# Split-operand gate and numerator products, a DRAM hop for the last gate chunk, and another order of the first weights in a two-layer hybrid trunk

## The chip, the core and the metric

The kernel runs on one core of a Trainium2 chip. The metric is the device time of one execution in microseconds (us), taken as the median of several runs. TensorE (PE) does the matrix products, VectorE (DVE) and ScalarE (ACT) the elementwise work, GpSimd (POOL) some elementwise work and the issue of some transfers, SyncE (SP) issues most transfers. All arrays are float32 in DRAM.

## What is computed

The reference is a trunk of two layers over 256 tokens of width 2048. Cut to what matters here:

```python
for i in range(2):
    hn = rmsnorm(h, norm[i])
    if i == 0:                                   # even layer
        qa, fa, ia, za, xb, zb = split(hn @ e_w_in)
        ya = head_rmsnorm(hgrn2(qa, fa, ia, lb), a_norm) * silu(za)
        xc = causal_conv(xb, b_conv_w, b_conv_b)
        r  = sigmoid(blockwise(xc, w_r) + b_r)   # 8 blocks of 128x128
        ig = sigmoid(blockwise(xc, w_i) + b_i)
        a  = exp(-8 * r * softplus(-lam))
        yb = scan(a, sqrt(1 - a * a) * (ig * xc)) * silu(zb)
        mix = concat(ya, yb) @ e_w_out
    else:                                        # odd layer, mLSTM with 8 heads
        qk, v, og, z, ig, fg = split(hn @ o_w_in)
        q, k = silu(causal_conv(qk))
        num = (q k^T * weights) @ v ; den = row sums of (q k^T * weights)
        yc = head_rmsnorm(num / den, c_norm) * sigmoid(og) * silu(z)
        mix = yc @ o_w_out
    h = h + mix
    h = h + sigmoid(h @ ple_gate_w[i]) * rmsnorm(p[i] @ ple_w[i], ple_norm[i])
out = rmsnorm(h, final_norm)
```

The "gates" of the change are the products of xc with w_r and w_i. The "numerators" are num, with den as one column more.

## The kernel before

**The large products.** TensorE takes float32 operands in two ways here. Plain float32 tiles are multiplied as they are. The large projections instead split each operand into a rounded part `hi` and the rest `lo`, both of type fp32r, and add three products, hi hi + hi lo + lo hi. `load_weights` (L119) fetches a half megabyte (128x1024) at a time into `raw` (5 buffers), casts it on ACT into `whi` (L131) and subtracts on VectorE into `wlo` (L132); whi and wlo have 4 buffers each, and a quarter of a chunk of weights is two such halves. Activations are split in the same way into tiles tagged `ahl` (12 buffers).

`block` (L154) makes one 128-feature block of an even-layer projection, features on partitions: 16 matmuls of 512 columns (L161) and 16 of 256 columns (L167). `quarter_tok` (L214) makes a quarter of a 512-column chunk, tokens on partitions: for each of two token halves 12 matmuls of 512 columns (L225 to L227). `project_tok` runs the four quarters of a chunk; `chunks` and `project_two` (L199, L209) run the first two chunks of a projection in the order (0,0) (0,1) (0,2) (1,0) (1,1) (1,2) (0,3) (1,3), chunk first, quarter second, and call `before(kq)` ahead of each; `ready` (L406) then steps the generator that makes activations 2kq and 2kq+1 until they exist.

**The order of the side work.** All else is written as Python generators in named lanes. `start` puts one into a lane, `step` runs it to its next `yield`, `drain` to its end. `pump` (L74) steps every lane once; it is called in the middle of each `block` and each quarter, so a yield is worth one block or quarter (about 5.5 us). What a pump issues is queued behind the latest matmul, cast and subtraction on their engines. A framework orders the instructions of each engine by priority and sets the semaphores; the casts and subtractions of weights have a raised priority.

**The parts that are touched.**

- Start: `embed` (L317) multiplies p by the first embedding weights. Its first half megabyte comes in four pieces, its second in two, alternating between the queues of ACT and SP; the third and fourth come whole on SP's queue. Then follow the parameters, and x in four chunks of half a megabyte (`load_x`, L479), each scaled and split by ACT (L286) and VectorE (L287), and the weights of the first projection (`in_ei`). The embedding's results are copied out of PSUM into `pl` (L347, L349).
- Gates: `rg_lru` (L809) runs twice (r = 0, 1), in a lane of its own. It loads 128x1024 gate weights `bw`, yields, and then issues 8 plain float32 matmuls a half (L823), four to a yield, each read by a sigmoid.
- Mixer gate of the even layer: `feature_major` (L515) takes a gated chunk from tokens to features: two VectorE transposes of 32x32 blocks (L520), a write to DRAM and four reads back on POOL's queue (`across`, L504, with `lag` yields), and copies on ACT and splits. The odd layer uses it for the first three of four chunks; the last goes through `feature_major_pe` (L531) with 8 TensorE transposes (L542), and all four are drained before the output projection `out_proj` (L413) begins.
- Numerators: `mix(j)` (L1038) runs for four pairs of heads. It makes the weights `wt` (from a pool of 4 tiles of 128x1024, `room`), the scores (L1058, L1059) times these weights in a second tile `scw`, and then the plain float32 products with v (L1070, L1072), with a column of ones as the 257th for den.

Of the kernel before, what the change touches and what calls it, by code (L numbers as in the profile page):

```python
# [11 lines left out]
F32 = mybir.dt.float32  # L12
# [31 lines left out]
def trunk(ctx: ExitStack, tc: tile.TileContext, a, out):  # L44
# [73 lines left out]

    def load_weights(src, pieces=(1, 1), queues=(sy,)):  # L119
        parts = []  # L120
        for hf in range(2):
            raw = wp.tile([P, 1024], F32, name="raw", tag="raw", bufs=5)
            hi = wp.tile([P, 1024], F32R, name="whi", tag="whi")
            lo = wp.tile([P, 1024], F32R, name="wlo", tag="wlo")
            n = 1024 // pieces[hf]
            for c in range(0, 1024, n):
                r, h, l = (x[:, c:c + n] for x in (raw, hi, lo))
                queues[c // n % len(queues)].dma_start(out=r, in_=src[:, hf * 1024 + c:hf * 1024 + c + n])
                with ExitStack() as order:
                    order.enter_context(tc.high_priority(offset=400))  # L130
                    last["act"] = s.copy(h, r).ins  # L131
                    last["dve"] = v.tensor_tensor(out=l, in0=r, in1=h.bitcast(F32), op=ALU.subtract).ins  # L132
            parts.append((hi, lo))
        return parts
# [379 lines left out]

    def feature_major(u, gain, first, y, room):  # L515

        w = room("w")
        w5 = w.rearrange("p (j c h t) -> p h c j t", j=4, c=4, h=2)
        for hf in range(2):
            v.transpose(w5[:, hf], u[:, hf].rearrange("p (c j q) -> p c j q", c=4, j=4))  # L520
        r = room("r")
        yield from across(w, r, f"du{gain}{first}", 5)
        r5 = r.rearrange("p (i c h t) -> p c h i t", i=4, c=4, h=2)
        for b in range(2):
            x = tp.tile([P, 512], F32, name="xr", tag="hn", bufs=3)
            for k in range(2):
                s.activation(x[:, k * T:(k + 1) * T].rearrange("p (h i t) -> p h i t", h=2, i=4), r5[:, 2 * b + k],
                             AF.Copy, scale=pc(gain, first + 2 * b + k))
            y[first // 2 + b] = split_act(x, "y")

    def feature_major_pe(u, gain, first, y):  # L531

        yield
        yield
        banks = []
        for b in range(2):
            ps = px.tile([P, 512], F32, name="mx", tag="mx")
            for k in range(2):
                c = (2 * b + k) * P
                for hf in range(2):  # L540
                    o = k * T + hf * P
                    te.transpose(ps[:, o:o + P], u[:, hf, c:c + P], ident)  # L542
            banks.append(ps)
        yield
        for b, ps in enumerate(banks):
            hi, lo, both = act_pair()
            for k in range(2):
                scaled_split(ps[:, k * T:(k + 1) * T], gain, first + 2 * b + k, hi[:, k], lo[:, k])
            y[first // 2 + b] = (hi, lo, both)

# [54 lines left out]
    with m0_scope:  # L605
# [203 lines left out]
        def rg_lru(r, xc):  # L809
# [6 lines left out]
            if r:  # L816
                yield
            for j in range(2):
                for w, (dst, bias) in enumerate(((av, "bbr"), (it, "bbi"))):
                    ps = px.tile([P, 512], F32, name="mx", tag="mx")  # L820
                    for i in range(2):
                        c = 2 * j + i
                        te.matmul(ps[:, i * T:(i + 1) * T], bw[:, w, c * P:(c + 1) * P], xc[:, c * T:(c + 1) * T],  # L823
                                  start=True, stop=True)
                    for i in range(2):
# [90 lines left out]
    drain("pl")  # L916
    act = out_proj(hq, a["eo"], y, "fe")
    drain("pg")
# [29 lines left out]
    with tc.tile_pool(name="m1", bufs=2) as m1:  # L948
# [38 lines left out]

        VW = 257
        vts = []
# [48 lines left out]
        def mix(j):  # L1038
# [24 lines left out]
            vt = vts[j]  # L1063
            nm = m1.tile([P, 2, 512], F32, name="num", tag="vt", bufs=6)
            for i in range(2):
                pool, tag = ((px, "mx"), (pst, "st"))[i]
                for hf in range(2):
                    c = hf * 8 + 2 * j + i
                    ps = pool.tile([P, 512], F32, name="nu", tag=tag)[:, 0:VW]
                    te.matmul(ps, scw[:, i, hf * P:(hf + 1) * P], vt[:, 0, i], start=True, stop=(hf == 0))  # L1070
                    if hf:
                        te.matmul(ps, scw[:, i, T:384], vt[:, 1, i], start=False, stop=True)  # L1072
                    o = nm[:, hf, i * 256:(i + 1) * 256]
                    s.copy(o, ps[:, 0:256])
                    v.tensor_copy(den[:, c:c + 1], ps[:, 256:VW])
                    sq = tp.tile([P, 512], F32, name="sq", tag="sq")[:, 0:256]
# [19 lines left out]
        for j in range(4):  # L1096
            psv = project_tok(a["ov"], j, acth)
            vt = m1.tile([P, 2, 2, VW], F32, name="vt", tag="vt", bufs=6)
            gp.memset(vt[:, :, :, 256:VW], 1.0)
            for hf in range(2):  # L1100
                s.activation(vt[:, hf, :, 0:256], psv[hf].rearrange("p (i e) -> p i e", i=2), AF.Copy,
                             scale=norm["rt"][:, hf:hf + 1])
            vts.append(vt)
            for c in (j // 2, 2 + j // 2):
                drain(f"qk{c}")
            start("mix", mix(j))
# [15 lines left out]
        for j in range(4):  # L1122
            u = m1.tile([P, 2, 512], F32, name="u", tag="vt", bufs=6)
            gate_tok(a["oz"], j, acth, u)
            for hf in range(2):
                for i in range(2):
# [234 lines left out]
```

## Time and profile before

| | |
|---|---|
| Median of 3 runs | 1051.79 us (1050.85 to 1053.89) |
| The profiled execution's own time | 1051.14 us |
| Its span, first to last instruction | 1049.4 us |
| Granted TensorE clock | 0.998 |
| Moved by DMA | 225.40 MB, mean 215 GB/s |

The profile comes from one execution. Its views: the busy time of each engine; the chain of work that ended last, followed back from the last instruction; groups of instructions by line, operation and tile, with busy time and mean duration; the waits; a timeline; the busy time of each engine in given stretches. Times are us from the first instruction. PE and PEld are TensorE's matmuls and its weight loads, a trailing q an engine's sequencer. Matmuls overlap, so the durations of single matmuls add up to more than the time they take.

### The profile page before, as it was taken

How to read it: one execution, taken by the hardware profiler on the slowest of the kernel's cores; microseconds unless marked ns; L12 is line 12 of the kernel's file. 1: busy time of each engine (PE TensorE's matmuls, PEld its weight loads, DVE VectorE, ACT ScalarE, POOL GpSimd, SP SyncE). 2: the span in 40 equal slices, each digit the busy share in tenths (PEclk: the TensorE clock that was granted, in tenths of full speed). 3: DMA queues.
4: the chain of work that ended last, by engine and by line, in shares of the span. 5: the costliest groups of instructions: out<-in, count | busy, mean ns of one | idle time of the engine just before them, and what ended most of it. 6: DMA issues, size and time to landing. Idle time of an engine off the chain costs nothing.

```text
span 1049.4 us, 14961 instructions
## 1 busy us (share of the span) xinstructions
PE 1038.6 (99%) x5504; PEld 869.1 (83%) x5504; DVE 724.3 (69%) x1085; ACT 594.3 (57%) x893; POOL 114.4 (11%) x162
## 2 busy tenths in 40 slices
PE   9999999999999999999999999999999999999996
PEld 7888888888888888887888788888888888888886
DVE  6857897997877666766569864454457767666675
ACT  7775545869654444565557765544445565444553
POOL 0001232522201111111021000000001110111000
PEclk9999999999999999999999999999999999999999
DMA  9865544545867877687597644446557775977652
GB/s 350 311 205 192 172 164 157 182 150 192 275 234 258 249 247 230 212 277 235 177 271 248 203 169 160 161 161 201 199 188 225 250 262 187 294 239 242 201 181 81
DMA packets 64587, 225.40 MB, mean 215 GB/s; under 512 B 8065, under 2 KB 9345, under 8 KB 64513
## 3 DMA queue, kind: packets, MB, share of 16 engines
q1 hardware_dynamic: 55440, 196.38, 56.5%
q0 software_dynamic: 8496, 27.27, 8.6%
q8 instruction: 43, 0.70, 0.3%
q10 hardware_dynamic: 576, 0.79, 0.2%
q14 instruction: 32, 0.25, 0.1%
HBM read 211.30 MB, written 13.11 MB: 214 GB/s over the span
## 4 chain that ended last, share of the span: by engine, by line
PE 97%; DMA 1%; ACT 1%; DVE 0%; issue 0%; SPq 0%; ACTq 0%
PE mm L225 22%; PE mm L226 22%; PE mm L227 22%; PE mm L161 11%; PE mm L167 6%; PE mx L225 2%; PE mx L227 2%; PE mx L226 2%; PE mm L338 1%; DMA xq<-in_xT_dram 1%; PE mm L1196 1%; PE mm L1195 1%; PE mm L1194 1%; PE mx L823 1%; PE nu L1070 1%; PE mx L661 0%
## 5 line engine op out<-in xcount | busy, mean ns | idle before, releaser
L132 DVE TENSOR_TENSOR wlo<-raw,whi 128x1024 fp32r<-128x1024 f32 (+1 forms) x364 | 439.9, 1220 | 246.4 <-ACT whi L131 211.3
L131 ACT CAST whi<-raw 128x1024 fp32r<-128x1024 f32 (+1 forms) x364 | 378.3, 1043 | 356.4 <-PE mm L227 254.8
L225 PE MATMUL mm<-whi,ahl 128*128 128x512 f32 x1024 | 401.5, 392 | 0.0
L227 PE MATMUL mm<-whi,ahl 128*128 128x512 f32 x1024 | 398.5, 389 | 0.0
L226 PE MATMUL mm<-wlo,ahl 128*128 128x512 f32 x1024 | 398.4, 389 | 0.0
L225 PEld LDWEIGHTS mm<-whi,ahl 128*128 128x128 f32 x1024 | 192.2, 188 | 42.0 <-issue 2.1
L227 PEld LDWEIGHTS mm<-whi,ahl 128*128 128x128 f32 x1024 | 192.2, 188 | 40.5
L226 PEld LDWEIGHTS mm<-wlo,ahl 128*128 128x128 f32 x1024 | 192.3, 188 | 39.8 <-DVE wlo L132 0.5
L161 PE MATMUL mm<-ahl,whi 128*128 128x512 f32 x512 | 122.1, 390 | 0.0
L161 PEld LDWEIGHTS mm<-ahl,whi 128*128 128x128 f32 x512 | 94.2, 188 | 18.3
L167 PE MATMUL mm<-ahl,wlo 128*128 128x256 f32 x512 | 67.7, 285 | 0.0
L167 PEld LDWEIGHTS mm<-ahl,wlo 128*128 128x128 f32 x512 | 64.9, 191 | 2.2
L225 PE MATMUL mx<-whi,ahl 128*128 128x512 f32 x96 | 37.5, 391 | 0.0
L227 PE MATMUL mx<-whi,ahl 128*128 128x512 f32 x96 | 37.4, 389 | 0.0
L226 PE MATMUL mx<-wlo,ahl 128*128 128x512 f32 x96 | 37.3, 389 | 0.0
L507 POOL DMA_DIRECT2D ducn<-w x3 | 1.7, 561 | 206.2 <-DVE w L520 206.2
L173 ACT COPY sm<-mm 128x256 f32<-128x256 f32 x32 | 11.7, 366 | 19.1 <-PE mm L167 19.0
L225 PEld LDWEIGHTS mx<-whi,ahl 128*128 128x128 f32 x96 | 18.0, 188 | 3.7
L227 PEld LDWEIGHTS mx<-whi,ahl 128*128 128x128 f32 x96 | 18.0, 188 | 3.8
L226 PEld LDWEIGHTS mx<-wlo,ahl 128*128 128x128 f32 x96 | 18.0, 188 | 3.7
L971 DVE SCALAR_TENSOR_TENSOR qk<-xr,prm,qk 128x255 f32<-128x255 f32 (+2 forms) x48 | 20.4, 475 | 0.6 <-ACT qk L968 0.5
L1195 PE MATMUL mm<-wlo,ahl 128*128 128x256 f32 x64 | 18.1, 283 | 0.0
(304 smaller groups left out, 877.3 us busy)
## 6 DMA issues: line engine op xcount, KB each, us to landing
raw<-in_ew_dram SPq DMA_DIRECT2D x64, 512.0 KB, 4.4
raw<-in_g_dram SPq DMA_DIRECT2D x56, 512.0 KB, 4.7
raw<-in_eo_dram SPq DMA_DIRECT2D x32, 512.0 KB, 4.8
raw<-in_oqk_dram SPq DMA_DIRECT2D x32, 512.0 KB, 4.6
raw<-in_ov_dram SPq DMA_DIRECT2D x32, 512.0 KB, 3.8
raw<-in_oog_dram SPq DMA_DIRECT2D x32, 512.0 KB, 3.7
raw<-in_oz_dram SPq DMA_DIRECT2D x32, 512.0 KB, 4.2
raw<-in_oo_dram SPq DMA_DIRECT2D x32, 512.0 KB, 4.5
```

The costliest lines, as they stand in the source:

```text
L131: last["act"] = s.copy(h, r).ins
L132: last["dve"] = v.tensor_tensor(out=l, in0=r, in1=h.bitcast(F32), op=ALU.subtract).ins
L161: last["pe"] = te.matmul(ps, parts[k // 8][0][:, c:c + P], act[k // 2][2][:, (k % 2) * 512:(k % 2 + 1) * 512], start=(k == 0), stop=False).ins
L167: last["pe"] = te.matmul(ps[:, T:2 * T], parts[k // 8][1][:, c:c + P], act[k // 2][0][:, k % 2], start=False, stop=(k == KT - 1)).ins
L173: s.copy(small, ps[:, T:2 * T])
L225: te.matmul(ps[hf], xh, wh, start=(k == 0), stop=False)
L226: te.matmul(ps[hf], xh, wl, start=False, stop=False)
L227: last["pe"] = te.matmul(ps[hf], xl, wh, start=False, stop=(k == KT - 1)).ins
L338: last["pe"] = te.matmul(ps[hf], tokens(pact[x], k, hf), (hi, lo)[y][:, k * 512:(k + 1) * 512], start=(n == mine[0]), stop=(n == mine[-1]) ...
L823: te.matmul(ps[:, i * T:(i + 1) * T], bw[:, w, c * P:(c + 1) * P], xc[:, c * T:(c + 1) * T], start=True, stop=True)
L971: v.scalar_tensor_tensor(dst[:, sh:T], pi[:, 0:T - sh], pc("ccw", k * 16 + n), dst[:, sh:T], op0=ALU.mult, op1=ALU.add)
L1195: te.matmul(ps[hf], xh, wl, start=False, stop=False)
```

## The change

- Gates: the gate weights are split into a whi and a wlo tile and xc into two ahl tiles, with one yield more, and each product becomes three (`mm3`, L149).
- Numerators: scores are written over `wt`; their split goes into two tiles of the same pool; v is split as it leaves PSUM (`vl` in an ahl tile), and the width becomes 258; each product becomes three, the third with 256 columns.
- The last gate chunk of the odd layer goes through `feature_major`, like the others; `feature_major_pe` goes. The output projection of the odd layer runs through `chunks` and `ready`, in place of a drain of all four.
- `feature_major` gets a `lag`. The even layer uses 4, with a yield ahead of its transposes; the odd layer keeps 5.
- First weights: pieces 0 and 1 on ACT's queue, pieces 2 and 3 and the second half megabyte on SP's, and the third half megabyte in two pieces.

```diff
-    def load_weights(src, pieces=(1, 1), queues=(sy,)):
+    def load_weights(src, pieces=(1, 1), queues=8 * (sy,)):
...
-                queues[c // n % len(queues)].dma_start(out=r, in_=src[:, hf * 1024 + c:hf * 1024 + c + n])
+                queues[hf * 4 + c // n].dma_start(out=r, in_=src[:, hf * 1024 + c:hf * 1024 + c + n])
...
-            parts = load_weights(w[b], *(((4, 2), (s, sy)) if head else ()))
+            parts = load_weights(w[b], *((((4, 2), (s, s) + 6 * (sy,)) if head else ((2, 1),)) if first else ()))
...
-    def out_proj(hq, w, y, lane):
+    def out_proj(hq, parts, lane):
...
-        for c in range(4):
-            ps = project_tok(w, c, y)
+        for c, ps in enumerate(parts):
...
-    def feature_major(u, gain, first, y, room):
+    def feature_major(u, gain, first, y, room, lag):
 
+        if lag < 5:
+            yield
         w = room("w")
...
-        yield from across(w, r, f"du{gain}{first}", 5)
+        yield from across(w, r, f"du{gain}{first}", lag)
...
-    def feature_major_pe(u, gain, first, y):
...
+            bh, bl = (wp.tile([P, 2, 512], F32R, name=n, tag=n) for n in ("whi", "wlo"))
+            s.copy(bh, bw)
+            v.tensor_tensor(out=bl, in0=bw, in1=bh.bitcast(F32), op=ALU.subtract)
+            xs = [split_act(xc[:, j * 512:(j + 1) * 512], "xc") for j in range(2)]
+            yield
             for j in range(2):
...
-                        te.matmul(ps[:, i * T:(i + 1) * T], bw[:, w, c * P:(c + 1) * P], xc[:, c * T:(c + 1) * T],
-                                  start=True, stop=True)
+                        mm3(ps[:, i * T:(i + 1) * T], bh[:, w, c * P:(c + 1) * P], bl[:, w, c * P:(c + 1) * P], xs[j], i,
+                            True, True)
...
-                start(f"fm{g}", feature_major(u, "an", 4 * g, y, room0))
+                start(f"fm{g}", feature_major(u, "an", 4 * g, y, room0, 4))
...
-    act = out_proj(hq, a["eo"], y, "fe")
+    act = out_proj(hq, (project_tok(a["eo"], c, y) for c in range(4)), "fe")
...
-            scw = room("scw")[:, 0:768].rearrange("p (i t) -> p i t", i=2)
...
-                v.scalar_tensor_tensor(scw[:, i, :], sc[:, 0:384], SC, wt[:, i, :], op0=ALU.mult, op1=ALU.mult)
+                v.scalar_tensor_tensor(wt[:, i, :], sc[:, 0:384], SC, wt[:, i, :], op0=ALU.mult, op1=ALU.mult)
+            sh, sl = (bp.tile([P, 1024], F32R, name=n, tag="wt")[:, 0:768].rearrange("p (i t) -> p i t", i=2)
+                      for n in ("sh", "sl"))
+            s.copy(sh, wt)
+            v.tensor_tensor(out=sl, in0=wt, in1=sh.bitcast(F32), op=ALU.subtract)
             yield
...
-                    te.matmul(ps, scw[:, i, hf * P:(hf + 1) * P], vt[:, 0, i], start=True, stop=(hf == 0))
-                    if hf:
-                        te.matmul(ps, scw[:, i, T:384], vt[:, 1, i], start=False, stop=True)
+                    for b, o in ((0, hf * P), (1, T))[:1 + hf]:
+                        for x, y, n in ((sh, vh, VW), (sl, vh, VW), (sh, vl, T)):
+                            te.matmul(ps[:, 0:n], x[:, i, o:o + P], y[:, b, i], start=(b == 0 and x is sh and y is vh),
+                                      stop=(b == hf and y is vl))
...
+            vl = ap.tile([P, 1024], F32R, name="vl", tag="ahl").rearrange("p (h i e) -> p h i e", h=2, i=2)
...
+                v.scalar_tensor_tensor(vl[:, hf], src, norm["rt"][:, hf:hf + 1], vt[:, hf, :, 0:256].bitcast(F32),
+                                       op0=ALU.mult, op1=ALU.subtract)
...
-            start(f"fm{j}", feature_major(u, "cn", 4 * j, y, room) if j < 3 else feature_major_pe(u, "cn", 4 * j, y))
+            start(f"fm{j}", feature_major(u, "cn", 4 * j, y, room, 5))
...
-        drain("fm0", "fm1", "fm2", "fm3")
+        step("fm3")
         start("emb", embed_norm())
-        act = out_proj(hq, a["oo"], y, "fo")
+        act = out_proj(hq, chunks(a["oo"], 4, y, ready(y, "fm")), "fo")
```

More of the change, by code (lines that the diff above doesn't have):

```diff
@@ L529, in feature_major @@
             y[first // 2 + b] = split_act(x, "y")
-    def feature_major_pe(u, gain, first, y):
[L533 to L549, printed above, removed]
     def gate_tok(w, j, act, u):
@@ L986, in trunk @@
             step(f"qk{j}")
-        VW = 257
+        VW = 258
         vts = []
@@ L1097, in trunk @@
             psv = project_tok(a["ov"], j, acth)
-            vt = m1.tile([P, 2, 2, VW], F32, name="vt", tag="vt", bufs=6)
-            gp.memset(vt[:, :, :, 256:VW], 1.0)
+            vt = m1.tile([P, 2, 2, VW], F32R, name="vt", tag="vt", bufs=6)
+            gp.memset(vt.bitcast(F32)[:, :, :, 256:VW], 1.0)
+            vl = ap.tile([P, 1024], F32R, name="vl", tag="ahl").rearrange("p (h i e) -> p h i e", h=2, i=2)
             for hf in range(2):
-                s.activation(vt[:, hf, :, 0:256], psv[hf].rearrange("p (i e) -> p i e", i=2), AF.Copy,
-                             scale=norm["rt"][:, hf:hf + 1])
-            vts.append(vt)
+                src = psv[hf].rearrange("p (i e) -> p i e", i=2)
+                s.activation(vt[:, hf, :, 0:256], src, AF.Copy, scale=norm["rt"][:, hf:hf + 1])
+                v.scalar_tensor_tensor(vl[:, hf], src, norm["rt"][:, hf:hf + 1], vt[:, hf, :, 0:256].bitcast(F32),
+                                       op0=ALU.mult, op1=ALU.subtract)
+            vts.append((vt, vl))
             for c in (j // 2, 2 + j // 2):
```

4 lines of the change are left out of this document (2 added, 2 removed).

## Prediction

> **What bounds the kernel now.** I read the busy shares first, then the chain of work that ended last.
>
> ```profile
> span 1049.4 us, 14961 instructions
> ## 1 busy us (share of the span) xinstructions
> PE 1038.6 (99%) x5504; PEld 869.1 (83%) x5504; DVE 724.3 (69%) x1085; ACT 594.3 (57%) x893; POOL 114.4 (11%) x162
> ```
>
> ```profile
> PE 97%; DMA 1%; ACT 1%; DVE 0%; issue 0%; SPq 0%; ACTq 0%
> ```
>
> TensorE is busy 99% and the chain is TensorE for 97%: from 17.87 us to the tail one matmul follows another. The waits of TensorE hold one wait of a weight matmul in the whole run, in the start:
>
> ```profile
> PE mm L338 <- DVE wlo L132: 0.6, 1, 0.6
> ```
>
> So three things can move the end: the work on TensorE, the start before 17.87 us, and a new stall. A matmul's duration in the groups (285 ns below) is latency, and the matmuls overlap; what one costs is its share of a run in the chain, which I call the pitch.
>
> **The change part by part: gates.** The chain around the gate matmuls of the RG-LRU (L823), whose two columns are start and length, and the groups kept apart by shape:
>
> ```profile
> 192.34 1.92 PE mx L823 x8
> 194.27 1.91 PE mm L167 x16
> 196.17 3.65 PE mm L161 x16
> 199.83 1.73 PE mx L823 x8
> ...
> 241.45 1.73 PE mx L823 x8
> ```
>
> ```profile
> L1070 PE MATMUL nu<-vt,scw 128*128 128x257 f32 x32 | 8.2, 379 | 0.0
> L823 PE MATMUL mx<-xc,bw 128*128 128x256 f32 x32 | 7.7, 382 | 0.0
> ```
>
> ```profile
> L1072 PE MATMUL nu<-vt,scw 128*128 128x257 f32 x16 | 4.8, 379 | 0.0
> ```
>
> The code issues 16 gate matmuls (2 halves r, 2 pairs j, 2 gates, 2 blocks i) and the trace has 32 records: a plain f32 matmul is two records, each 1.73 / 8 = 0.216 us, so 0.432 us for one. Four runs of 8 records; the first is 0.19 longer, coming after the 32-wide matmuls of L661, and I take that 0.19 as a switch which the next matmul pays in any case. Cost now: 4 x 1.73 = 6.92 us. After: 16 x 3 = 48 products of split operands with 256 columns. L167 is just that, with weights loaded anew each time:
>
> ```profile
> L167 PE MATMUL mm<-ahl,wlo 128*128 128x256 f32 x512 | 67.7, 285 | 0.0
> ```
>
> and its run above gives 1.91 / 16 = 0.1194 us. 48 x 0.1194 = 5.73 us. **Gain 1.19 us.** Three products are cheaper than one f32 matmul only because that takes two records of nearly twice this pitch.
>
> **Numerators.** One of four chunks, in the chain:
>
> ```profile
> 642.59 0.87 PE nu L1070 x4
> 643.46 0.43 PE nu L1072 x2
> 643.89 0.87 PE nu L1070 x4
> 644.76 0.43 PE nu L1072 x2
> ```
>
> 2.60 us a chunk, 10.40 for four: 48 records, 24 matmuls. After: 24 x 3 products, 48 of them with 258 columns, 24 with 256. From L161 (3.65 / 16 = 0.228 for 512 columns) and L167, a column costs 0.1087 / 256 = 0.0004 us, so 258 columns 0.1203: 48 x 0.1203 + 24 x 0.1194 = 8.64 us. **Gain 1.76 us.** No row has 258 columns; the bounds are 0.1194 and, if the odd width cost as much as 512, 0.228 (5.2 us worse). I take 0.1203, two columns from a row that is shown.
>
> **Last gate chunk by DRAM.** The transposes at L542 go:
>
> ```profile
> 853.12 5.62 PE mm L338 x24
> 858.75 0.44 PE mx L542 x4
> 859.19 5.50 PE mm L338 x24
> 864.69 0.44 PE mx L542 x4
> ```
>
> **Gain 0.88 us**, as they stand in the chain. What takes their place: two VectorE transposes, one DRAM write and four reads on POOL's queue, and four ACT copies with two splits. The chunk's gated tile is complete near 858 (its last products follow the matmuls that end at 853.12), and with the order of quarters (0,0) (0,1) (0,2) (1,0) (1,1) (1,2) before (0,3), features 6 and 7 are read only after the rest of the embedding and six quarters of 24 x 0.228 = 5.47 us: 865 + 33 = 898. The generator ends one pump earlier than the same code does in the gate of the even layer, which stalls nowhere. If that cover were gone, the hop would show, a write and four reads side by side, by the last column (us from issue to landing) of
>
> ```profile
> ducn<-w POOLq DMA_DIRECT2D x3, 512.0 KB, 3.3
> r<-ducn POOLq DMA_DIRECT2D x12, 128.0 KB, 5.8
> ```
>
> 9.1 us. What comes later than before is the chunk before it (features 4 and 5), finished in the pump of (0,1) and read 12 matmuls, 2.7 us, later; the even layer's gate again has that same distance. I cost it at nothing. The split of the scores adds a 128x768 copy and subtraction, some 0.75 and 0.95 us (three quarters of the casts quoted below, an estimate), and the split of v two subtractions a chunk. Scores and numerators are one quarter apart, 5.47 us, and the weights of a quarter take 2 x 0.95 us of ACT and 2 x 1.24 of VectorE: both fit. The v subtraction holds a PSUM bank longer, but that bank is wanted 12 matmuls later at the earliest. I cost these at nothing; rival 4 is what they cost uncovered.
>
> **The start.** The chain's first rows, and TensorE's timeline:
>
> ```profile
> 5.16 8.10 DMA xq<-in_xT_dram
> 13.34 0.51 ACT ahl L286
> 13.85 0.47 ACT pl L349
> 15.04 0.57 ACT pl L349
> 15.61 0.95 ACT whi L131
> 16.59 1.24 DVE wlo L132
> 17.87 0.50 PE mm L226
> ```
>
> ```profile
> 5.08 2.52 PE L338 MATMUL mx<-whi,ahl 128*128 128x512 f32 x8
> ```
>
> ```profile
> 12.04 0.50 PE L338 MATMUL mm<-wlo,ahl 128*128 128x512 f32 x1 [0.58 <-DVE wlo L132]
> ```
>
> 48 embedding matmuls and one of L225 need 49 x 0.228 = 11.17 us from 5.08, so could end at 16.25; L226 starts at 17.87. Gaps: 1.62 us, the most that the new order of first weights can give. The 0.58 at 12.04 is a wait for the third half megabyte, which comes in two pieces after the change: that wait goes. But what is late next is the first x chunk, landing at 13.26, and ACT, which is full from 13.34 on with two pl copies ahead of the cast. SP's queue gets three transfers more ahead of x (two first pieces trade places, the first half of the second half megabyte leaves ACT's queue, and the third becomes two), but the bytes ahead of x are the same, so its landing stays. Gain from below nothing (-0.1, one more transfer's issue) to 1.62. If one pl copy gets ahead of the landing, 0.47 is saved: I take 0.47, the nearest row. The Trainium skill, DMA: Bandwidth & Descriptors, "Issuing engines are not separate DMA queues", says that another issuing engine saves only issue time. By that the change of queue itself gives nothing, and with a gain of 0 here the sum would be 0.47 us less; the rest of the text does not need this.
>
> **What the splits of the gates could stall.** The weights of a gate half (128x1024) are split into the pool of whi and wlo (4 buffers, two quarters of weights) and stay there for two pumps; a copy of 0.95 us (as the cast at 15.61) and two of 0.57 go to ACT; a subtraction of 1.24 (as at 16.59) and two of half its width, some 0.65 each by that row, 2.5 us together, go to VectorE, behind which the next wlo waits, and TensorE for it. VectorE, ACT and POOL busy (third, fourth and fifth entry after the length) in the two stretches, then the tightest wlo of that part and the matmul that reads it:
>
> ```profile
> 205.00:210.00 5.00, 5.00 (x91) 4.31 (x90) 3.10 (x7) 4.96 (x8) 1.62 (x2) 1.00 0.73 269
> 240.00:245.00 5.00, 5.00 (x30) 4.45 (x30) 1.87 (x10) 4.97 (x21) 0.72 (x1) 1.00 0.57 208
> ```
>
> ```profile
> 219.75 3.21 DVE L132 TENSOR_TENSOR wlo<-raw,whi 128x1024 fp32r<-128x1024 f32 x2
> ```
>
> ```profile
> 222.58 0.39 PE L226 MATMUL mm<-wlo,ahl 128*128 128x512 f32 x1
> ```
>
> The pair ends at 222.96 and its second takes 1.24, so the first ends near 221.7, some 0.8 us before 222.58. VectorE has 1.90 us free in 205 to 210 and 3.13 in 240 to 245; 2.5 us more overrun the first by 0.6, just under that 0.8. So perhaps nothing; the other bound is worked out in the rivals (+8.2). I take +0.3 as next to nothing. The later transposes (one pump later, one wait less, same last pump) are hidden by four pumps of 5.5 us for a hop of 9.
>
> **Sum.** 1.19 + 1.76 + 0.88 + 0.47 - 0.30 = 4.00 us off. The profiled execution took 1051.14 us (span 1049.4): 1047.14. The median of the runs, 1051.79, is 0.65 above it, so 1047.8.
>
> **The rivals.**
>
> 1. VectorE loses the race for its operands (rests on these rows):
>
> ```profile
> 246.16 4.07 DVE L132 TENSOR_TENSOR wlo<-raw,whi 128x1024 fp32r<-128x1024 f32 x2
> ```
>
> ```profile
> 246.47 2.67 POOL L797 TENSOR_TENSOR o<-o,hnr 128x1024 f32<-128x1024 f32 x1
> ```
>
> Two subtractions of 1.24 us took 4.07 beside a POOL product: 1.6 more. If the new ones meet POOL in both halves, each makes TensorE 1.6 + 0.6 - 0.8 = 1.4 us late: 2.8 in place of 0.3, so 1050.3. For it: the second half's split is issued in the pump that reads out the attention, whose end is this product. Against: VectorE has free time after 210. The Trainium skill, SBUF — State Buffer, "SBUF: two separate sides", says that VectorE, with two SBUF inputs, and GpSimd lock a shared pair of ports for a whole instruction and the loser blocks; the 4.07 us agree.
>
> 2. Slower: the copy of the gate weights heads ACT's queue before a whi buffer is free. A buffer comes free when the first half of a quarter has been used, 18 of 24 matmuls or 4.1 us in; ACT stands, and casts and the reading out of PSUM stand behind it. Twice 4.1 = 8.2 us, against 4.30 gained by the other terms: 3.9 over the median, 1055.7. It decides once ACT stands longer than the weights are ahead, at most a quarter of 5.47 us with four buffers and half of that with three. Against: copies are queued where the buffer is due.
>
> 3. The start closes wholly: 1.62 in place of 0.47, so 1046.6. For it: the third half megabyte is TensorE's only recorded wait. Against: ACT is full from 13.34.
>
> 4. The numerators pay for width or wait for the split scores: up to 5.2 more, or four times half a us: 1049.8 to 1053.0. Against: the rows of L161 and L167 lie on a line.
>
> That the start gives nothing at all, since x decides, is 1048.3, inside the forecast's own range.
>
> **How the numbers follow.** Forecast 0.50 (1046.9 to 1048.7), rival 1 0.20, rival 2 0.07, rival 3 0.15, rival 4 0.08. About 0.3%, 3.2 us, is what a measurement of this kernel tells from no change: faster is under 1048.6, slower over 1054.9. Faster: 0.45 of the forecast and all of rival 3, 0.60. Slower: rival 2 and a little of 4, 0.08. Within: 0.32. The range goes from 1046.2 (rival 3) to 1051.0 (rival 1 with 0.7 over it); outside are rival 2, half of 4 and the lower end of 3.
>
> **What would show it.** Gates: 48 records of 256 columns at a pitch of 0.119 in the chain, about 5.7 us in all. Numerators: 72 records, 2.16 us a chunk. No transposes between the embedding's matmuls. The first L226 at 17.4, not 17.87, with no wait at 12.04. New rows in TensorE's waits between 195 and 262 would be rivals 1 and 2 (for a wlo, or for a whi or an ACT read of PSUM), at 610 to 700 rival 4. The forecast is wrong if TensorE's chain has holes there longer than 0.5 us, or if a product of 258 columns is far from 0.12.

## The result and the profile after

The changed kernel takes 1046.15 us (median of 6 runs, 1045.51 to 1046.38). Beside it the kernel before took 1051.36 us in 6 runs; the ratio is 0.9943, 95% interval 0.9931 to 0.9956. The forecast was 1047.8 us and its range began at 1046.2, so the gain is larger than the range allowed. Later runs of the kernel before, five groups of 10 to 33, have medians of 1050.30 to 1050.53 us: the 1051.79 of the first three runs was high. All six runs of the first comparison lie at 1050.85 or above, where only 29 of 116 later ones do, so this was hardly the luck of three draws; what made that kernel slower there was not found. Against 1050.4 the change gives about 4.25 us. One execution in the experiments ran at a granted clock of 0.752 (1292.47 us) and is left out of every comparison.

The page of the changed kernel, its span, busy times and the shares of the chain:

```profile
span 1043.9 us, 15076 instructions
## 1 busy us (share of the span) xinstructions
PE 1034.5 (99%) x5536; PEld 867.9 (83%) x5536; DVE 736.5 (71%) x1104; ACT 597.6 (57%) x904; POOL 113.3 (11%) x167
...
PE 99%; ACT 0%; issue 0%; DVE 0%; ACTq 0%; POOL 0%; POOLq 0%
```

TensorE has 32 matmul records more and is busy 4 us less; VectorE has 12 us more to do and still hides it. The waits of TensorE now hold only the first one of the run, before any weight has arrived; the 0.6 at L338 is gone, but it is also absent from the second profile of the kernel before (before_again, below):

```profile
PE st L95 <- POOL ones L90: 1.1, 1, 1.1
```

Where the time went is read by the starts of the same weight matmuls in two traces. The table gives the distances between them, for two profiled executions of the kernel before (the first is the one that the prediction read) and one of the kernel after:

| stretch (us in the kernel before) | before, first | before, second | after |
|---|---|---|---|
| start, up to a matmul near 25 | 25.03 | 24.46 | 24.08 |
| both gate halves, 189.6 to 271.5 | 81.96 | 81.96 | 81.04 |
| numerators, 614 to 703 | 89.18 | 89.18 | 87.30 |
| second embedding, last chunk, 853 to 886 | 32.91 | 32.73 | 31.73 |
| from the start of the last matmul to the end | 9.10 | 9.14 | 8.62 |
| all else | 811.17 | 811.19 | 811.17 |
| span | 1049.35 | 1048.66 | 1043.94 |

Against the second execution: 0.38 + 0.92 + 1.88 + 1.00 + 0.52 = 4.70 of the 4.72 us. Three rows are near what was forecast, one (the tail, from the last matmul's start) was nowhere in the sum, and the first row differs as much between two executions of one kernel as between the kernels. Without the first row the stages give 4.32, near the 4.25 of the medians.

**Numerators and gates.** The groups of the numerators, kept apart by shape, and one chunk of them in the chain:

```profile
L1061 PE MATMUL nu<-vt,sl 128*128 128x258 f32 x24 | 6.8, 282 | 0.0
L1061 PE MATMUL nu<-vt,sh 128*128 128x258 f32 x24 | 6.8, 282 | 0.0
L1061 PE MATMUL nu<-vl,sh 128*128 128x256 f32 x24 | 6.8, 282 | 0.0
```

```profile
640.23 2.14 PE nu L1061 x18
```

2.14 / 18 = 0.119 us: 258 columns cost as 256 do. In the chain around the first gate half, the matmuls of L642 are those that stood at L661 before:

```profile
190.57 0.82 PE mx L642 x64
191.39 2.10 PE mm L167 x16
193.49 3.65 PE mm L161 x16
197.14 0.12 PE mx L150
...
198.46 0.12 PE mx L152
198.57 1.92 PE mm L167 x16
```

Twelve products from 197.14 to 198.57 are 0.119 each. The extra 0.19 us of the switch, which the gate matmuls paid before, is now in the 2.10 of L167 (1.92 further down), as forecast. One piece of the second half is longer than its pitch of 0.23:

```profile
242.06 0.23 PE mm L227
242.28 0.23 PE mm L225
242.51 0.41 PE mm L226
```

That 0.18 is a subtraction of VectorE that comes late: the view of the matmuls' waits has no row for it, but the weight load of this L226 sat idle for 0.3 us until the `wlo` of L132 was there. What the gates with the later transposes lose against the 1.19 of their products is 0.27 in all.

### The profile page after: what moved, and what is told of

The parts are those of the page before. It is cut to its first block, busy times and chain, and to the rows that moved or that the text cites. A ratio compares the mean times of both kernels' runs of the same rounds, so it can differ in the third digit from the quotient of the medians.

```text
span 1043.9 us, 15076 instructions
## 1 busy us (share of the span) xinstructions
PE 1034.5 (99%) x5536; PEld 867.9 (83%) x5536; DVE 736.5 (71%) x1104; ACT 597.6 (57%) x904; POOL 113.3 (11%) x167
## 4 chain that ended last, share of the span: by engine, by line
PE 99%; ACT 0%; issue 0%; DVE 0%; ACTq 0%; POOL 0%; POOLq 0%
PE mm L225 22%; PE mm L226 22%; PE mm L227 22%; PE mm L161 11%; PE mm L167 6%; PE mx L227 3%; PE mx L226 3%; PE mx L225 3%; PE mm L338 2%; PE nu L1061 1%; PE mm L1189 1%; PE mm L1188 1%; PE mm L1187 1%; PE mx L642 0%; PE st L95 0%; PE mx L764 0%
## 5 line engine op out<-in xcount | busy, mean ns | idle before, releaser
L132 DVE TENSOR_TENSOR wlo<-raw,whi 128x1024 fp32r<-128x1024 f32 (+2 forms) x365 | 438.1, 1212 | 235.1 <-ACT whi L131 201.8
L131 ACT CAST whi<-raw 128x1024 fp32r<-128x1024 f32 (+2 forms) x365 | 378.9, 1041 | 333.1 <-PE mm L227 220.8
L225 PE MATMUL mm<-whi,ahl 128*128 128x512 f32 x992 | 387.9, 391 | 0.0
L226 PE MATMUL mm<-wlo,ahl 128*128 128x512 f32 x992 | 386.3, 389 | 0.0
L227 PE MATMUL mm<-whi,ahl 128*128 128x512 f32 x992 | 386.2, 389 | 0.0
L225 PEld LDWEIGHTS mm<-whi,ahl 128*128 128x128 f32 x992 | 186.3, 188 | 40.5 <-issue 2.1
L226 PEld LDWEIGHTS mm<-wlo,ahl 128*128 128x128 f32 x992 | 186.3, 188 | 38.8 <-DVE wlo L132 0.8
L227 PEld LDWEIGHTS mm<-whi,ahl 128*128 128x128 f32 x992 | 186.2, 188 | 38.9
L167 PE MATMUL mm<-ahl,wlo 128*128 128x256 f32 x512 | 67.3, 284 | 0.0
L167 PEld LDWEIGHTS mm<-ahl,wlo 128*128 128x128 f32 x512 | 64.8, 191 | 2.0
L225 PE MATMUL mx<-whi,ahl 128*128 128x512 f32 x128 | 50.0, 391 | 0.0
L227 PE MATMUL mx<-whi,ahl 128*128 128x512 f32 x128 | 49.8, 389 | 0.0
L226 PE MATMUL mx<-wlo,ahl 128*128 128x512 f32 x128 | 49.8, 389 | 0.0
L225 PEld LDWEIGHTS mx<-whi,ahl 128*128 128x128 f32 x128 | 24.0, 188 | 5.0
L226 PEld LDWEIGHTS mx<-wlo,ahl 128*128 128x128 f32 x128 | 24.0, 188 | 5.0
L227 PEld LDWEIGHTS mx<-whi,ahl 128*128 128x128 f32 x128 | 24.0, 188 | 5.0
```

The lines of the kernel that those rows point to most:

```text
L167: last["pe"] = te.matmul(ps[:, T:2 * T], parts[k // 8][1][:, c:c + P], act[k // 2][0][:, k % 2], start=False, stop=(k == KT - 1)).ins
L225: te.matmul(ps[hf], xh, wh, start=(k == 0), stop=False)
L226: te.matmul(ps[hf], xh, wl, start=False, stop=False)
L227: last["pe"] = te.matmul(ps[hf], xl, wh, start=False, stop=(k == KT - 1)).ins
```

## The experiments

In the expectations, theory A is that the gains stand in the stages of their parts and add up, and the other letters are the rivals to it that each expectation spells out.

**One part at a time.** Four kernels, each the kernel before with one part of the change (the edits are cut to the lines that matter): only the first weights; only the gates with the later transposes; only the numerators; only the last chunk with the order of the projection after it.

```diff
head:  + parts = load_weights(w[b], *((((4, 2), (s, s) + 6 * (sy,)) if head else ((2, 1),)) if first else ()))
gates: + mm3(ps[...], bh[...], bl[...], xs[j], i, True, True)    and feature_major(u, "an", 4 * g, y, room0, 4)
nums:  + for x, y, n in ((sh, vh, VW), (sl, vh, VW), (sh, vl, T)):    with VW = 258
lastc: + start(f"fm{j}", feature_major(u, "cn", 4 * j, y, room))
       + act = out_proj(hq, chunks(a["oo"], 4, y, ready(y, "fm")), "fo")
```

> The kernel before with the new first weights alone (queues and the third half megabyte in two). Theory A (the parts add, each with the step that the two traces show at its place; the half us in the tail belongs to none): 0.98 us faster, the first L226 near 16.9 instead of 17.87, x landing near 12.3 instead of 13.26, tail after the last matmul 9.1 as before. Rival B (x landed early in that one execution by chance, and only the order on ACT is new): 0.5 us faster, x near 13.2. Rival C (the shorter tail comes from the start, since all is earlier): 1.5 us faster, tail 8.6.

> The kernel before with the three-product gates alone, with the later transposes of the even mixer gate, which they need. Theory A: 0.92 us faster: 48 products at 0.119 us against 32 records at 0.216 give 1.19, and 0.2 to 0.3 us of it is lost in short waits and switches near 195 to 262. Rival: the whole 1.19 shows, and the lost part in the changed kernel came from the other edits. Rival C: 1.4 or more, if the tail's half us comes with it.

> The kernel before with the three-product numerators alone. Theory A: 4 steps of 0.46 us, 1.84 us faster, no wait at the numerators. Rival: the sum of my pitches, 1.76, or less if a product of 258 columns costs more than its width, which the steps would show.

> The kernel before with the last gate chunk through DRAM and the output projection by chunks alone. Theory A: 1.14 us faster: the 0.88 of 16 transposes' records in the chain and 0.26 more, since the first split matmuls behind plain float32 ones also start late. Rival: 0.88 and no more, if the 0.26 came from another edit. Rival C: 1.6, if the tail's half us comes with it.

Measured beside a median of 1050.35 of the kernel before: head 1050.40 (ratio 1.0, 0.9991 to 1.0009), gates 1049.65 (0.9994, 0.9985 to 1.0003), nums 1048.59 (0.998, 0.9972 to 0.9989), lastc 1049.08 (0.9986, 0.9977 to 0.9995). The gains are -0.05 + 0.70 + 1.76 + 1.27 = 3.68 us, less than the 4.25 of the whole, although three of the four hold the tail's half us (below), which the whole has once. Each of the four is uncertain by about 0.9 us, so the sum settles little, and the stages of the profiled executions are read instead. In nums the numerators' stretch gives the full 1.88, but 0.79 is lost in the second embedding and 0.13 ahead of the numerators. Its waits have a row that the whole change does not have:

```profile
PE mm L338 <- ACT pl L349: 0.5, 1, 0.5
```

The chain of nums in that place, start and length of each piece:

```profile
841.43 6.27 DMA r<-ducn
...
847.86 1.31 ACT xr L527 x3
...
851.18 1.24 ACT whi L131 x2
...
853.67 0.47 ACT pl L349
...
854.19 3.03 PE mm L338 x12
```

ACT stands until 847.70 for the third chunk's way through DRAM, then works off its copies, splits and casts, and the copy that frees a bank for the embedding comes late. A stall of one engine in the middle of its queue so shows up at another line 6 us later.

The numerators need not be the cause. Here are ACT's first copies of that chunk, which follow the landing, in nums, in the execution of the kernel before that the prediction read, and in its second execution:

```profile
847.86 1.31 ACT L527 ACTIVATE xr<-r,prm 128x256 f32<-128x256 f32 x3 [1.22 <-DMA r<-ducn]
```

```profile
849.39 1.31 ACT L527 ACTIVATE xr<-r,prm 128x256 f32<-128x256 f32 x3 [0.61 <-DMA r<-ducn]
```

```profile
848.18 1.31 ACT L527 ACTIVATE xr<-r,prm 128x256 f32<-128x256 f32 x3
```

The chunk's last read landed 3.12, 3.74 and 4.38 us ahead of the embedding's first matmul, and the second embedding's stretch is 33.52, 32.91 and 32.73. So it is in all nine profiles with the old path of the last chunk: 32.73 where the landing is 4.38 us ahead or more, 32.86 to 32.91 where it is 3.74 to 3.76, and 33.52 in nums. The write to DRAM was issued at the same place in all of them, 15.9 us ahead of that matmul; in nums it took 4.27 us to land, in both executions of the kernel before 3.26, in the two kernels with gates alone 3.94 and 3.98, and the reads behind it vary as well. So the 0.79 goes with one late landing. The kernel before loses 0.18 in the same way when its landing is late; that the numerators made the landing later is not shown. The profiled execution of nums (1049.19) was also 0.6 us slower than its median.

**Repeats, and the start taken out.** The kernel after again, the kernel before against itself, the whole change with the old first weights, and the old order with only the third half megabyte in two.

```diff
nohead:     parts = load_weights(w[b], *(((4, 2), (s, sy)) if head else ()))
head_split: + (4, 2), (s, sy, s, sy, s, sy, sy, sy)   and   (2, 1) for the second weights
```

> The changed kernel once more, beside more runs of the kernel before. Theory A (the parts add; the 5.2 us of the first comparison holds one us of a kernel before that ran late): the sum of the parts' steps, head 0, gates 0.95, numerators 1.84, last chunk 1.14, so 3.9 us faster, ratio 0.9963, with the kernel before near 1050.4. Rival D (the parts help one another, since the numerators alone lost 0.6 us at the last gate chunk and the start alone gave nothing): 5.2 us, ratio 0.995.

> The kernel before against itself, for how far two profiles and two medians of one program lie apart. Theory A: medians within 0.3 us of each other; in this profile x lands at 11.9 to 12.6 and the first L226 starts at 17.1 to 17.6, so that 13.26 and 17.87 of the first profile were late. Rival D: x at 13.2 and L226 at 17.9 again, and the early landings in the kernels with one part came from their edits.

> The changed kernel with the old first weights. Theory A: the same time as the changed kernel within 0.3 us (the new start gave nothing alone). Rival E (the start is paid only once the rest is quicker, or its 0.98 us in the aligned traces is real): 0.5 to 1.0 us slower than the changed kernel.

> The kernel before with only the third half megabyte in two pieces; queues and order as before. Theory A: no change of time within 0.3 us; the wait for the third half megabyte near 12 us goes, TensorE ends the embedding earlier and then waits for the split of the first projection weights. Rival: the split alone brings L226 to 17.0 and 0.5 us, and the new queues take it back.

Measured beside 1050.53: after_again 1046.13 (0.9953, 0.9937 to 0.997), before_again 1050.65 (0.9998, 0.9988 to 1.0008), nohead 1046.17 (0.9953, 0.9935 to 0.997), head_split 1050.47 (0.9998, 0.9987 to 1.0009). The start gives nothing that the medians show, alone or in the whole. The chain's first pieces of after and then of before_again, an execution of the unchanged kernel:

```profile
5.30 3.03 PE mx L338 x12
8.33 8.41 PE mm L338 x36
16.74 0.23 PE mm L225
16.97 0.26 PE mm L226
```

```profile
5.31 3.76 PE mx L338 x12
9.07 8.26 PE mm L338 x36
17.33 0.23 PE mm L225
17.55 0.26 PE mm L226
```

TensorE's timeline has the start of the first L226 itself, in before_again and then in after:

```profile
17.39 0.43 PE L226 MATMUL mm<-wlo,ahl 128*128 128x512 f32 x1
```

```profile
16.81 0.42 PE L226 MATMUL mm<-wlo,ahl 128*128 128x512 f32 x1
```

17.39 where the prediction's trace had 17.87 and where 17.4 was forecast for the changed kernel: the old code reaches that forecast by itself when x comes sooner. x landed at 13.26 us in the execution that the prediction read, and at 11.8 to 12.6 in the nine others up to here. Between the second profiles, before_again and after_again, the new order is 0.4 us ahead at the matmul near 25. But over all profiles the two orders overlap there: 24.2 to 25.0 us in ten with the old order, 24.1 to 24.6 in seven with the new one.

**The later transposes, which were costed at nothing.** The gates alone, and then the whole change, each with the even layer's transposes where they were.

```diff
-                start(f"fm{g}", feature_major(u, "an", 4 * g, y, room0, 4))
+                start(f"fm{g}", feature_major(u, "an", 4 * g, y, room0, 5))
```

> Three-product gates alone, with the even layer's transposes where they were (no later transposes). Theory A: the later transposes are hidden by four pumps, so the time is that of the gates with them, 1049.65, the gates' stages give the same 0.9 us against before, and the wait of some 0.2 us at the L226 near 242.7 stays, because it comes from the split of the second half of the gate weights on VectorE. Rival: the later transposes are what gives or takes part of it; then the stages differ by 0.2 us or more, or a wait shows near 262 to 300, in the output projection of the even layer. The tail is 8.65 by theory F (ACT has about 1354 instructions).

> The kernel after with the even layer's transposes where they were before the change (a lag of 5, no yield ahead of them); all else stays. Theory J (the splits of the second gate half fill VectorE, and the later transposes keep 1.2 us of two chunk transposes out of that place): as in the gates without later transposes, one wait of a product L226 for the subtraction L132 of about 1.1 us near 242.5, span 1.1 to 1.2 us longer than the kernel after, median near 1047.3. Rival (the wait of 1.1 us belongs to the gates alone, since in the whole change other parts move VectorE's work): no such wait, 1046.15.

> The kernel after without the later transposes once more, for its profile (the first try's profile was taken at a granted clock of 0.752 and shows no chain that can be compared; its median over the other runs is 1047.12, 1.0 above the kernel after). Theory J: one wait of L226 for L132 of about 1.1 us near 242.5, and everything else as in the kernel after. Rival: no such row, and the 1.0 us spread over many places or in the start.

> The kernel after without the later transposes once more, for its profile (the first try's profile was taken at a granted clock of 0.752 and shows no chain that can be compared; its median over the other runs is 1047.12, 1.0 above the kernel after). Theory J: one wait of L226 for L132 of about 1.1 us near 242.5, and everything else as in the kernel after. Rival: no such row, and the 1.0 us spread over many places or in the start.

Measured: gates_nolag 1050.45 beside 1050.40 (1.0001, 0.9992 to 1.0009), so without the later transposes the three-product gates give nothing; after_nolag 1047.12 (0.9967, 0.9955 to 0.998), 0.97 above the kernel after. The profile is that of after_nolag_look (1047.43). Theory A failed for gates_nolag, J held. The waits of after_nolag_look, and the matmul that waited, in TensorE's timeline:

```profile
PE mm L226 <- DVE wlo L132: 1.4, 2, 1.1
```

```profile
244.09 0.50 PE L226 MATMUL mm<-wlo,ahl 128*128 128x512 f32 x1 [1.12 <-DVE wlo L132]
```

VectorE's timeline there, and after it the same place of the kernel after:

```profile
236.46 1.22 DVE L801 TENSOR_TENSOR wlo<-bw,whi 128x1024 fp32r<-128x1024 f32 x1
...
239.33 0.68 DVE L146 TENSOR_TENSOR ahl<-xc,ahl 128x512 fp32r<-128x512 f32 x1
239.93 0.68 DVE L872 TENSOR_TENSOR u<-u,o 128x512 f32<-128x512 f32 x1
240.53 1.30 DVE L521 STREAM_TRANSPOSE wu<-u 128x512 f32<-128x512 f32 x2
...
242.82 1.22 DVE L132 TENSOR_TENSOR wlo<-raw,whi 128x1024 fp32r<-128x1024 f32 x1
```

```profile
235.98 1.22 DVE L801 TENSOR_TENSOR wlo<-bw,whi 128x1024 fp32r<-128x1024 f32 x1
...
238.85 0.68 DVE L146 TENSOR_TENSOR ahl<-xc,ahl 128x512 fp32r<-128x512 f32 x1
239.45 0.69 DVE L872 TENSOR_TENSOR u<-u,o 128x512 f32<-128x512 f32 x1
...
241.15 1.22 DVE L132 TENSOR_TENSOR wlo<-raw,whi 128x1024 fp32r<-128x1024 f32 x1
...
242.36 0.70 DVE L521 STREAM_TRANSPOSE wu<-u 128x512 f32<-128x512 f32 x1
```

VectorE is nearly full from 236 to 245 in both (busy 8.86 and 8.83 of 9 us). Without the move, two transposes, 1.30 us together, stand ahead of the subtraction that TensorE needs, and it starts at 242.82 and not at 241.15; 0.48 of these 1.67 us is that this execution is that much later already at the L801 shown. With the move the transposes come behind it. The stretch of the gates is 1.21 us longer without it (82.25 against 81.04).

**The tail.** The last 0.5 us has no work of the change in it, and yet every kernel with gates, numerators or last chunk in it had the short tail (8.61 to 8.69) in the first ten profiles, and the others the long one (9.10 to 9.14). The difference in the traces is one packet of 8192 bytes on q14, a queue of the kind "instruction" (so it is read here as a fetch of instructions), 5.9 us after the start of the last matmul, between the last stores of the output. The queues of the last microseconds (packets, MB, share), before_again and then after:

```profile
q1 hardware_dynamic: 1186, 1.72, 51.4%
q10 hardware_dynamic: 144, 0.26, 7.7%
q14 instruction: 1, 0.01, 0.2%
```

```profile
q1 hardware_dynamic: 1146, 1.70, 56.7%
q10 hardware_dynamic: 144, 0.26, 8.5%
```

In all ten profiles the last such packet, wherever it falls, starts when ACT has begun 1338 to 1345 of its recorded instructions, waits and transfers counted; the kernel before has 1347, gates 1354, the kernel after 1368. So padding was tried: 8 tiny copies on ACT, or on VectorE, in the middle of the kernel before, and 107 on ACT in the kernel after, to bring its count 128 above 1347.

```diff
pad_act:   + 90 <= len(pumps) < 98 and s.copy(scr, eps); pumps.append(1)
pad_dve:   + 90 <= len(pumps) < 98 and v.tensor_copy(scr, eps); pumps.append(1)
after_pad: + 40 <= len(pumps) < 147 and s.copy(scr, eps); pumps.append(1)
```

> The kernel before with 8 ACT copies of 128x1 added in eight successive pumps of the middle, beside work of TensorE; nothing of the change is in it. Theory F (the tail's half us is a fetch of instructions): in every profile so far the last 8192-byte packet of the instruction queue starts when ACT has begun 1338 to 1345 of its recorded instructions; with 1347 in all that is in the tail, 5.9 us after the last matmul starts, and with 1351 or more it is ahead of the last matmul. With 8 more it comes some 2 to 4 us ahead of the last matmul, the tail from the last matmul's start to the end of the span is 8.6 to 8.7 us, not 9.1, and the median is about 0.45 us under the kernel before. Rival G (the half us comes from what the parts of the change do, their products or hops): tail 9.1, median the same. Rival H (any longer program does it, whatever the engine): tail 8.65 here and with the padding on VectorE.

> The kernel before with 8 VectorE copies of 128x1 in the same eight pumps. Theory F: ACT keeps 1347 instructions, the packet of 8192 bytes stays in the tail at 5.9 us, tail 9.1, median the same as before. Rival G: the same. Rival H: tail 8.65, 0.45 us faster.

> The kernel after with 107 ACT copies of 128x1 added, one in each of 107 successive pumps; ACT then has 1368 + 107 = 1475 recorded instructions, 128 more than the kernel before. Theory F: fetches come every 128 instructions, so one falls near instruction 1472 and is in the tail again: tail 9.1 us instead of 8.62, median 0.45 us above the kernel after, 1046.6; the matmuls ahead of the tail stand within 0.1 us, since ACT has the room. Rival G: tail 8.6, time as after. If the 107 copies delay reads of PSUM or casts, new waits of TensorE show and the time rises further.

> The kernel after with 107 ACT copies of 128x1, placed so that all 107 are issued (of the first try only 95 were, which left ACT at 1463 recorded instructions, short of the 1472 at which the next fetch would fall). Theory F: ACT has 1475 recorded instructions, the last 8192-byte packet starts 5.9 us after the last matmul starts, the tail is 9.1 instead of 8.6 to 8.75, and the time is 0.35 to 0.45 us above the kernel after, 1046.6, beside what the copies themselves cost ahead of the tail. Rival G (the tail's half us belongs to what the parts of the change do): no packet in the tail, 8.6 to 8.75.

> The kernel after with 114 ACT copies of 128x1 (107 brought only 100 more recorded instructions, 1468, since seven waits on semaphores went away; the packet then came 10.5 us after the last matmul starts, behind the stores, and the tail was 8.76). With seven more, ACT has about 1475 recorded instructions, 128 more than the kernel before, whose fetch falls on the 1344th of 1347. Theory F: the packet of 8192 bytes starts 5.9 us after the last matmul, amid the stores, the last store packet ends near 7.6 instead of 7.05 to 7.2, the tail is 9.1 to 9.2, and the time is 0.3 to 0.5 us above that of the try with 107, 1046.76. Rival G: tail 8.6 to 8.76 whatever the count.

after_pad2 and after_pad3 have 107 and 114 copies, from the 60th pump on and more than one in some pumps. All copies were there in each; it is ACT's waits on semaphores that became fewer, so that the first two missed the count (the 95 in the expectation of after_pad2 is the count of recorded instructions, not of copies). Measured, times from the start of the last matmul:

| kernel | ACT, recorded | packet starts | last matmul to end | median |
|---|---|---|---|---|
| before_again | 1347 | +5.87 | 9.14 | 1050.65 |
| pad_dve | 1347 | +5.90 | 9.14 | 1050.34 |
| pad_act | 1354 | -2.67 | 8.86 | 1050.09 |
| after | 1368 | -13.03 | 8.62 | 1046.15 |
| after_pad | 1463 | none near | 8.76 | 1046.90 |
| after_pad2 | 1468 | +10.46 | 8.76 | 1046.76 |
| after_pad3 | 1475 | +5.92 | 9.12 | 1046.67 |

The last microseconds of after_pad3 have the packet again:

```profile
q14 instruction: 1, 0.01, 0.2%
```

after_pad3 differs from after_pad2 by seven copies alone, and in it the packet is back amid the stores. Theory F holds in the profiles, both ways: taken out of the tail of the kernel before, and put back into that of the kernel after, by nothing but the number of ACT's instructions. G and H fall. The size is 0.28 to 0.52 us, less beside padding, which costs 0.1 to 0.2 in the tail for a reason that stays open. The medians can't show it by themselves: pad_act has 0.9995 (0.9986 to 1.0004), pad_dve 0.9998 (0.9989 to 1.0007), and after_pad3 came out 0.09 below after_pad2, where 0.3 to 0.5 above was expected. The 107 or 114 copies also cost some 0.2 to 0.4 us near the mark of 40 us, which the padded kernels' half us over the kernel after holds too.

**Two parts together.** The numerators with the last chunk's part.

```diff
nums_lastc: the edits of nums and of lastc
```

> The three-product numerators together with the last chunk by DRAM and its order, nothing else of the change. Theory K (with the numerators alone, ACT stands behind the feature copies of the third chunk, which wait for DRAM, so that the reads of PSUM for the second embedding come late; the last chunk's part no longer asks for that chunk early): the wait of 0.5 us at L338 is gone, the numerators' stage gives 1.9, the last chunk's 1.0 to 1.2, the tail 0.45, so 3.4 under before, near 1047.0. Rival (the numerators' stall is their own, from the split of v and the scores): about 0.6 us less, 1047.6, with the wait at L338 still there.

Measured 1047.24 beside 1050.51 (0.9969, 0.9957 to 0.9981), between the two numbers; the waits decide:

```profile
PE st L95 <- POOL ones L90: 1.1, 1, 1.1
PE mx L338 <- ACT whi L131: 0.3, 1, 0.3
PE mm L338 <- DVE wlo L132: 0.3, 1, 0.3
```

Both waits of L338 here are in the start; the one for ACT's pl is gone, and the second embedding's stretch is 31.73, as in the whole change. As theory K said, the last chunk's part no longer asks for the third chunk early. The landing was even later here, 2.50 us ahead of the embedding's first matmul (1.90 in the kernel after), and cost nothing. What K says of the numerators is not shown: the kernel before has that wait too when its landing is late, 0.18 us in its first execution.

## Which step of the prediction failed, and what held

The forecast was 1.65 us above the result (1047.8 against 1046.15). The step that failed first is the base: "The median of the runs, 1051.79, is 0.65 above it, so 1047.8". That median of three was 1.4 us above the 1050.4 of the many later runs, from which the same 4.00 us would have given 1046.4. Why the early runs were slower stays open; of the 0.69 us between the two profiled executions of the kernel before, 0.57 is in the start and 0.18 in the second embedding.

The remaining 0.25 is the sum, and that it is so small is luck: the 0.47 of the start did not come, and a term of 0.52 in the tail came that the sum does not have.

- **Gates, 1.19, and the stall, -0.30:** together 0.89 forecast, 0.92 measured. The pitch, the place of the switch and the kind of the stall held: VectorE's queue, 0.2 of it left. But they hold only with the later transposes.
- **Later transposes, "hidden by four pumps":** the step that failed in mechanism. The hop was covered, as said, but the price of a step is also what it does to the queue that it stands in: moved, it keeps 1.2 us out of the gates. Without the move a loss near that of rival 1 (1.4 forecast for a half, a wait of 1.1 measured) comes about once, by VectorE's order and not beside a POOL product: the subtraction L132 takes 1.22 in both.
- **Numerators, 1.76:** 1.88. Width 258 costs nothing, and rival 4 did not come.
- **Last chunk, 0.88:** 1.00. "I cost it at nothing" held for the hop through DRAM. The prediction's view of TensorE's waits did not list that a weight load of the second embedding already waited 0.3 us for pl in the trace it read; the new order removes that exposure to a late landing.
- **Start, "I take 0.47":** nothing in the medians (head 1050.40 beside 1050.35, nohead 1046.17 against 1046.15). The row it was worked from was a late start: x at 13.26. "So its landing stays" was a statement about one draw of something that moves by 1.5 us. SP's queue got two transfers more ahead of x, not three: the first weights are five issues on it before and seven after. The Trainium skill, DMA: Bandwidth & Descriptors, "Issuing engines are not separate DMA queues", by which another issuing engine saves only issue time, agrees with these medians. Rival 3 (the start closes wholly) fell, though its number, 1046.6, came nearer than the forecast.
- **Tail, no term:** 0.52 in the profiles. The trace of before has the packet, but the prediction does not ask what the 9.10 us behind the last matmul consist of, because the change does not touch it.
- **Rival 2** (bh blocks ACT) has no row in any run.

## What to carry to other kernels

Take the base from as many runs as there are, and check a term that rests on a landing time against a second execution before giving it a price. When an edit adds work to an engine's queue, look for what else can be moved out of that queue at that place: the move can be worth as much as the edit. Parts are to be judged in the company that they will have: the gates without the later transposes lose all that they give. And a stall seen in one execution is to be looked for in other executions of the old kernel before it is put down to the edit: the one behind the numerators was a late landing, which the old kernel has as well.

## What the runs showed of the hardware

- A packet of 8192 bytes on the instruction queue falls near ACT's recorded instructions 1217, 1344 and 1472, so one for each 128 (64 bytes an instruction, by division). Between the last stores it lengthens the tail by 0.3 to 0.5 us, and the last store packet ends near 7.6 instead of 7.05 to 7.2 us after the last matmul's start.
- A split operand of 258 columns has the pitch of 256, 0.119 us; the loss of 0.19 us at a switch from 32-wide matmuls goes to whatever matmul follows.
- x, half a megabyte, issued at 5.0 to 5.7 us, lands between 11.8 and 13.3 us in 18 executions of the same or nearly the same code. The third chunk's write to DRAM, half a megabyte on POOL's queue, took 3.25 to 5.18 us to land in them.
